# Score pairs on one PSUM tile and matmul bursts in a two-layer hybrid attention block

## The chip, the cores and the metric

The kernel runs on one core of a Trainium2 chip. The metric is the device time of one execution in microseconds. Three runs before the change took 1876.28, 1876.46 and 1880.62 us; their median is 1876.46 us.

## The reference

Two layers work on 512 latent tokens and 256 context tokens of width 1024. A layer normalises and modulates both streams, multiplies them by one input matrix, and sends the parts through four groups of heads; their outputs are joined, multiplied by an output matrix and added, and a SwiGLU network follows. The second layer needs no context output. What matters here is the attention of three groups:

```python
# A: windowed attention, 4 query heads on 2 key heads of width 64, a sink column
p = softmax(concat([where(|q-k| <= 128, qa @ ka.T, -1e30), qa @ ka_ctx.T, sink]))
# C: differential attention, 4 heads, each with two maps m of query/key width 32
p0, p1 = softmax(q[:, m] @ concat([k, k_ctx])[:, m].T)  for m in (0, 1)
y = rmsnorm((p0 - lam * p1) @ concat([v, v_ctx]))
# D: neighbourhood attention on an 8 x 64 grid, 4 heads of width 64, with a bias table
p = softmax(concat([qd @ kd_near.T + bias, qd @ kd_ctx.T]))
```

Context tokens of the first layer run the same groups against the 256 context keys alone. Group B is a convolution of 31 taps.

## The kernel before, in words

Large products are made of three matmuls in a short format (`mm3`, lines 162 to 164: high x high, high x low, low x high). The scores are split in the same way: a chain of three matmuls for each group of columns (`mm_rows`, line 613; written out in `d_attn`, lines 785 to 788).

The score work comes in pairs of chains on different rows of the array. In group C (`c_attn`, line 623) a pair is the two maps of one head for 128 queries, on 32 rows each: per map three matmuls over 512 latent keys and three over 256 context keys (only the latter for context queries). In A (`a_attn`, line 817) and D (`d_attn`, line 769) a pair is two heads on 64 rows each. Each chain of a pair writes a PSUM tile of its own: `self.ps("sc")` (768 columns, two buffers) or `self.ps("sd")` (512 columns, two buffers), line 639, 717, 778 and 830. VectorE then reads each tile with one instruction that copies the scores to SBUF and takes the row minimum (line 648, 796, 845; `ctx_attn` takes the minimum alone, line 726). ScalarE makes the exponentials (line 651, 734, 799, 848). The weights are scaled or combined, turned on TensorE by `tr_copy` (line 498, copied back in line 509 or 512), and multiplied with V in `pv` (line 599): two heads, their matmuls alternating over key tiles, one PSUM tile of which each head writes 64 partitions.

The attention steps are generators. `beside` (line 924) runs an attention generator and takes steps of side work, mostly projections of the next group (`proj_c`, `proj_d`, `proj_a`, through `unit`, lines 389 to 415), between its steps. In this manner the program's order is C of layer 0 with the projections of C and D beside it (about 136 to 306 us), D with the projections of A (to about 402), A with the loads of the output matrix (to about 470), and the same in layer 1 from about 1195 to 1452. The first three units of group B are made in `first_units` (line 427), two of them in `sc` tiles.

The order on each engine is not the program's order. The framework plans it before the kernel is compiled: it replays the instructions on a simulated timeline, and each engine takes the lowest number among those that are ready, where the number is the place in the program. A PSUM tile is taken by the first writer that is let go, and is given back after its last reader. The planned order is then fixed; on the chip an engine that has reached an instruction waits for it. `tc.high_priority(n)` lowers the numbers of what is written inside it by n.

Other tiles play a part in the argument: in lines 1027 to 1037, at the start of layer 0, transposes of two normalised token tiles write two tiles of 1024 columns, two token tiles taking turns (`for kk in range(4): for j in range(2)`).

Of the kernel before, what the change touches and what calls it, by code (L numbers as in the profile page):

```python
# [16 lines left out]
P = 128  # L17
D = 1024
NK = D // P
SEQ = 512  # L20
CTX = 256
NT = SEQ + CTX
# [28 lines left out]
class Hybrid:  # L51
# [19 lines left out]
    def tl(self, pool, shape, tag, bufs=1, dt=F32):  # L71
# [5 lines left out]
        "t": {"pt": (512, 2)},  # L77
        "x": {"ps": (1024, 3)},
        "u": {"pu": (512, 2)},
        "c": {"sc": (768, 2)},  # L80
        "e": {"sd": (512, 2), "ptd": (512, 2)},
    }

    def ps(self, tag="ps"):
# [11 lines left out]

    def dma(self, out, in_):
        self.nc.sync.dma_start(out, in_)  # L98

    def small(self, w, tag, bufs=8):  # L100
        return self.tl(self.smp, [P, w], tag, bufs)
# [325 lines left out]
    def first_units(self, l, H, c0s, nctx, by_k, between):  # L427
        w = self.t["w_in"][l]
        ws = [self.w_unit(w, c0) for c0 in c0s]
        outs = []  # L430
        for n in range(len(c0s)):
            if n < 2:
                a = self.ps("sc")
                outs.append((a[:, 0:512], a[:, 512:768] if nctx else None))
            else:
                outs.append((self.ps("pu"), self.ps("pu")[:, 0:256] if nctx else None))
        groups = [(0, 0, 256), (0, 256, 512)] if not by_k else [(0, 0, 512)]
        if nctx:
            groups.insert(0, (1, CTX0, CTX0 + 256))
        for g in [groups] if by_k else [[g] for g in groups]:  # L440
            self.abreast(ws, [[o[1] if x else o[0][:, a:b] for x, a, b in g] for o in outs], H, g, by_k)
            if between:
                between()
                between = None
        self.first = dict(zip(c0s, outs))
# [153 lines left out]
    def pv(self, parts, dest):  # L599

        nc = self.nc
        po = self.ps(self.pv_tag)
        n = len(parts[0])
        for i in range(n):
            for j in range(2):
                v, pt = parts[j][i]
                nc.tensor.matmul(po[64 * j:64 * j + 64, 0:P], v, pt, start=(i == 0), stop=(i == n - 1))  # L607
        src = po[:, 0:P]
        if len(dest.shape) == 3:
            src = src.rearrange("p (r c) -> p r c", r=dest.shape[1])  # L610
        nc.scalar.copy(dest, src)

    def mm_rows(self, outs, qs, ks, rows):

        for i, (a, b) in enumerate(((0, 0), (0, 1), (1, 0))):
            for o, q, k, r in zip(outs, qs, ks, rows):
                self.nc.tensor.matmul(o, q[a][r], k[b][r], start=(i == 0), stop=(i == 2))  # L617

    def blk(self, PT, i):
        return PT[:, i * P:(i + 1) * P]  # L620
# [2 lines left out]
    def c_attn(self, l, u):  # L623
        nc = self.nc
        q_ = self.lay[l]
        if u == 0:
            self.nblk = 0
            self.L0 = self.tl(self.cpool, [P, 6, 4], "L0", 1)
        L0 = self.L0
        Q, K = self.qkc["q", u], self.qkc["k", u]  # L630
        for n in range(6 if l == 0 else 4):
            lat = n < 4
            w = NT if lat else CTX
            nb = w // P
            PT = []
            for j in range(2):
                h = 2 * u + j
                rows = [slice(64 * j + 32 * m, 64 * j + 32 * m + 32) for m in range(2)]
                pss = [self.ps("sc") for _ in range(2)]
                qs = [[a[:, n * P:(n + 1) * P] for a in Q]] * 2  # L640
                for c0, c1, o in ((0, 512, 0), (512, NT, 512)) if lat else ((512, NT, 0),):
                    self.mm_rows([ps[:, o:o + c1 - c0] for ps in pss], qs, [[a[:, c0:c1] for a in K]] * 2, rows)
                Pm = []
                lm = self.small(1, "l1")
                for m in range(2):
                    nm = self.small(1, "nm")
                    Pm.append(self.a_s())
                    nc.vector.tensor_tensor_reduce(out=Pm[m][:, 0:w], in0=pss[m][:, 0:w],  # L648
                                                   in1=self.zcol.to_broadcast([P, w]),
                                                   scale=1.0, scalar=HUGE, op0=ALU.add, op1=ALU.min, accum_out=nm)  # L650
                    nc.scalar.activation(Pm[m][:, 0:w], Pm[m][:, 0:w], AF.Exp, scale=-1.0, bias=nm,
                                         accum_out=L0[:, n, h:h + 1] if m == 0 else lm)
                rl = self.small(1, "rl")
                nc.vector.reciprocal(rl, lm)
                cf = self.small(1, "cf")
                nc.vector.scalar_tensor_tensor(cf, L0[:, n, h:h + 1], q_["nlam"], rl, op0=ALU.mult, op1=ALU.mult)
                self.nblk += 1
                if l or self.nblk % 2 == 0:
                    nc.scalar.activation(Pm[1][:, 0:w], Pm[1][:, 0:w], AF.Copy, scale=cf)
                    nc.gpsimd.tensor_tensor(Pm[0][:, 0:w], Pm[0][:, 0:w], Pm[1][:, 0:w], op=ALU.add)  # L660
                else:
                    nc.vector.scalar_tensor_tensor(Pm[0][:, 0:w], Pm[1][:, 0:w], cf, Pm[0][:, 0:w],
                                                   op0=ALU.mult, op1=ALU.add)
                PT.append(self.a_pt())
                self.tr_copy([Pm[0][:, b * P:(b + 1) * P] for b in range(nb)], PT[j])
                yield
            self.pv([[(self.VC[:, kb, (2 * u + j) * 64:(2 * u + j) * 64 + 64], self.blk(PT[j], kb - 6 + nb))
                      for kb in range(6 - nb, 6)] for j in range(2)], self.yg["C"][:, u, n * P:(n + 1) * P])
# [45 lines left out]
    def ctx_attn(self, Q, K, vts, sinks, dest, tag):  # L714

        nc = self.nc
        pss = [self.ps(tag) for _ in range(2)]
        kc = [[a[:, SEQ:NT] for a in K]] * 2
        for e in range(2):
            qs = [[a[:, SEQ + e * P:SEQ + (e + 1) * P] for a in Q]] * 2  # L720
            self.mm_rows([ps[:, e * 256:(e + 1) * 256] for ps in pss], qs, kc, self.HALVES)
        PT = []
        for ps, sinkn in zip(pss, sinks):
            S = self.a_s()
# [44 lines left out]
    def d_attn(self, l, pool, u):  # L769
        nc = self.nc  # L770
        vh = lambda tb, j: self.VD[:, tb, (2 * u + j) * 64:(2 * u + j) * 64 + 64]
        Q, K = self.qkd["q", u], self.qkd["k", u]
# [2 lines left out]
        dest = yv[:, 0:SEQ].rearrange("p (r g c) -> p g r c", r=8, g=4)  # L775
        v2 = lambda a: a.rearrange("p (a k) -> p a k", a=2)
        for g in range(4):
            pss = [self.ps("sd") for _ in range(2)]
            qs = [[a[:, g * P:(g + 1) * P] for a in Q]] * 2

            def win(a):
                if g:
                    return a[:, (g - 1) * P:(g + 1) * P]
                return bass.AP(a.tensor, a[:, 3 * P:4 * P].offset, ap=[list(a.ap[0]), [-3 * P, 2], [1, P]])
            for o, f in ((0, win), (256, lambda a: a[:, SEQ:NT])):
                for i, (x, y) in enumerate(((0, 0), (0, 1), (1, 0))):
                    for j, r in enumerate(self.HALVES):
                        nc.tensor.matmul(pss[j][:, o:o + 256], qs[j][x][r], f(K[y][r]), start=(i == 0), stop=(i == 2))  # L788
            ty = (0, 1, 1, 2)[g]
            PT = []  # L790
            for j in range(2):
                n0 = nbs[j][:, ty].rearrange("p b k c -> p (b k c)")
                bias = bass.AP(n0.tensor, n0.offset, ap=[list(n0.ap[0]), [(3 - ty) * 256, 2], [1, 256]])
                S = self.a_s()
                nm = self.small(1, "dnm")
                nc.vector.tensor_tensor_reduce(out=v2(S[:, 0:512]), in0=v2(pss[j][:, 0:512]), in1=bias,
                                               scale=1.0, scalar=HUGE, op0=ALU.add, op1=ALU.min, accum_out=nm)
                ls = self.small(1, "dls")
                nc.scalar.activation(S[:, 0:512], S[:, 0:512], AF.Exp, scale=-1.0, bias=nm, accum_out=ls)
                PT.append(self.a_pt())  # L800
                self.soft_dst(S, 512, ls, PT[j], self.tr_tag)
                yield
            tbs = ((3, 0), (0, 1), (1, 2), (2, 3))[g] + (4, 5)
            self.pv([[(vh(tb, j), self.blk(PT[j], s)) for s, tb in enumerate(tbs)] for j in range(2)], dest[:, g])
# [12 lines left out]
    def a_attn(self, l, x):  # L817
        nc = self.nc
# [3 lines left out]
        Q, K = self.qka["q", x], self.qka["k"]  # L822
        sinks = [q_["sinkn"][:, 2 * g + x:2 * g + x + 1] for g in range(2)]
        yv = self.yg["A"][:, x]
        for n in range(4):
            lo, hi = max(0, n - 1), min(3, n + 1)
            wl = (hi - lo + 1) * P
            w = wl + CTX
            qs = [[a[:, n * P:(n + 1) * P] for a in Q]] * 2
            pss = [self.ps("sc") for _ in range(2)]  # L830
            self.mm_rows([ps[:, 512 - wl:512] for ps in pss], qs, [[a[:, lo * P:(hi + 1) * P] for a in K]] * 2, self.HALVES)
            self.mm_rows([ps[:, 512:768] for ps in pss], qs, [[a[:, SEQ:NT] for a in K]] * 2, self.HALVES)
            PT = []
            for g in range(2):
                S = self.a_s()
# [543 lines left out]
```

## Time and profile before

| what | us |
|---|---|
| median of three runs | 1876.46 |
| profiled execution | 1877.07 |
| its span, first to last instruction | 1875.3 |
| TensorE busy (matmuls) | 1785.0 |
| VectorE, ScalarE, GpSimd busy | 905.2, 679.4, 432.1 |

The mean granted TensorE clock of the execution is 0.968 of full speed. Matmuls are pipelined: the record of one lasts longer than the time until the next may start, so busy times of single groups of matmuls add up to more than the stretch; the distance from a run's first start to the start of the next instruction is what it costs TensorE.

### The profile page before, as it was taken

How to read it: one execution, taken by the hardware profiler on the slowest of the kernel's cores; microseconds unless marked ns; L12 is line 12 of the kernel's file. 1: busy time of each engine (PE TensorE's matmuls, PEld its weight loads, DVE VectorE, ACT ScalarE, POOL GpSimd, SP SyncE). 2: the span in 40 equal slices, each digit the busy share in tenths (PEclk: the TensorE clock that was granted, in tenths of full speed). 3: DMA queues.
4: the chain of work that ended last, by engine and by line, in shares of the span. 5: the costliest groups of instructions: out<-in, count | busy, mean ns of one | idle time of the engine just before them, and what ended most of it. 6: DMA issues, size and time to landing. Idle time of an engine off the chain costs nothing.

```text
span 1875.3 us, 28384 instructions
## 1 busy us (share of the span) xinstructions
PE 1785.0 (95%) x11812; PEld 1499.4 (80%) x11812; DVE 905.2 (48%) x1435; ACT 679.4 (36%) x1161; POOL 432.1 (23%) x324
## 2 busy tenths in 40 slices
PE   6897999988999999999999999899998999999997
PEld 5676888866788788888888888788986888888886
DVE  4668554475344334242434247754366444544443
ACT  4354555455233121112121225565455242222322
POOL 1587612352000000000100004883262000000002
PEclk8897999978999999999999999999998999999999
DMA  9341201213505353424141221121114353322421
GB/s 314 81 128 36 53 23 35 88 45 96 180 13 170 120 154 104 135 70 126 57 125 42 85 79 46 51 55 40 46 54 132 117 169 101 110 82 79 128 75 46
DMA packets 187983, 172.88 MB, mean 92 GB/s; under 512 B 17878, under 2 KB 150478, under 8 KB 187726
## 3 DMA queue, kind: packets, MB, share of 16 engines
q1 hardware_dynamic: 187854, 171.06, 29.9%
q8 instruction: 93, 1.52, 0.4%
q14 instruction: 36, 0.29, 0.1%
HBM read 166.76 MB, written 4.52 MB: 91 GB/s over the span
## 4 chain that ended last, share of the span: by engine, by line
PE 81%; POOL 5%; DVE 5%; DMA 3%; issue 2%; ACT 2%; SPq 1%; POOLq 0%; DVEq 0%; ACTq 0%
PE ps L162 18%; PE ps L163 18%; PE ps L164 18%; PE sc L617 4%; POOL accp L873 3%; PE pu L162 3%; PE pu L163 3%; PE pu L164 3%; PE pt L498 3%; PE pt L607 3%; PE ada L292 2%; DVE accd L881 1%; PE pu L607 1%; SPq L98 1%; PE sd L788 1%
## 5 line engine op out<-in xcount | busy, mean ns | idle before, releaser
L163 PE MATMUL ps<-h,whi 128*128 128x512 f32 (+1 forms) x1104 | 383.0, 348 | 1.6 <-DVE h L129 1.6
L162 PE MATMUL ps<-h,whi 128*128 128x512 f32 (+1 forms) x1104 | 382.4, 349 | 0.9 <-DVE gt L980 0.9
L164 PE MATMUL ps<-h,wlo 128*128 128x512 f32 (+1 forms) x1104 | 383.0, 348 | 0.0
L127 ACT CAST whi<-wraw 128x1024 fp32r<-128x1024 f32 (+1 forms) x132 | 134.5, 1023 | 409.5 <-PE ps L163 252.5
L129 DVE TENSOR_TENSOR wlo<-wraw,whi 128x1024 fp32r<-128x1024 f32 (+1 forms) x116 | 147.8, 1278 | 202.0 <-ACT whi L127 200.7
L163 PEld LDWEIGHTS ps<-h,whi 128*128 128x128 f32 x1104 | 208.9, 189 | 28.4 <-DVE h L129 2.0
L162 PEld LDWEIGHTS ps<-h,whi 128*128 128x128 f32 x1104 | 207.8, 189 | 29.7 <-issue 2.8
L164 PEld LDWEIGHTS ps<-h,wlo 128*128 128x128 f32 x1104 | 208.8, 189 | 27.8 <-issue 2.2
L162 PE MATMUL pu<-hT,whi 128*128 128x256 f32 (+1 forms) x648 | 199.8, 309 | 11.1 <-DVE hp L575 4.2
L983 POOL TENSOR_TENSOR x<-x,gt 128x1024 f32<-128x1024 f32 x12 | 29.7, 2476 | 728.5 <-DVE gt L980 728.5
L163 PE MATMUL pu<-hT,whi 128*128 128x256 f32 (+1 forms) x648 | 197.5, 305 | 0.0
L164 PE MATMUL pu<-hT,wlo 128*128 128x256 f32 (+1 forms) x648 | 196.5, 303 | 0.0
L162 PE MATMUL ps<-wdhi,zh 128*128 128x512 f32 x440 | 171.6, 392 | 0.4 <-ACT ntmp L367 0.4
L163 PE MATMUL ps<-wdlo,zh 128*128 128x512 f32 x440 | 171.0, 390 | 0.0
L164 PE MATMUL ps<-wdhi,zl 128*128 128x512 f32 x440 | 170.4, 391 | 0.0
L873 POOL TENSOR_TENSOR accp<-accp,cpr 128x783 f32<-128x783 f32 (+1 forms) x76 | 143.3, 1885 | 31.8 <-ACT cpr L872 26.0
L980 DVE TENSOR_TENSOR gt<-ps,g 128x1024 f32<-128x1024 f32 x66 | 80.6, 1223 | 134.9 <-PE ps L164 116.2
L127 ACT CAST wdhi<-wraw 128x1024 fp32r<-128x1024 f32 x44 | 46.2, 1055 | 270.2 <-PE ps L164 180.9
L162 PEld LDWEIGHTS pu<-hT,whi 128*128 128x128 f32 x648 | 125.9, 194 | 22.4 <-DVE hp L575 4.8
L163 PEld LDWEIGHTS pu<-hT,whi 128*128 128x128 f32 x648 | 126.2, 195 | 7.2 <-issue 2.4
L164 PEld LDWEIGHTS pu<-hT,wlo 128*128 128x128 f32 x648 | 126.1, 195 | 6.2 <-issue 1.9
L617 PE MATMUL sc<-qk,qk 32*128 32x256 f32 (+3 forms) x648 | 112.9, 343 | 8.9 <-DVE nm L648 5.9
(270 smaller groups left out, 2983.0 us busy)
## 6 DMA issues: line engine op xcount, KB each, us to landing
araw<-in_w_ada SPq DMA_DIRECT2D x60, 512.0 KB
wraw<-in_w_gate SPq DMA_DIRECT2D x44, 512.0 KB
wraw<-in_w_up SPq DMA_DIRECT2D x44, 512.0 KB
wraw<-in_w_down SPq DMA_DIRECT2D x44, 512.0 KB
wraw<-in_w_in SPq DMA_DIRECT2D x40, 512.0 KB
wraw<-in_w_ada SPq DMA_DIRECT2D x20, 512.0 KB
wraw<-in_w_out SPq DMA_DIRECT2D x12, 512.0 KB
whi<-in_w_ada SPq DMA_DIRECT2D x8, 512.0 KB
```

Source lines behind the costliest of these rows:

```text
L127: nc.scalar.copy(hi, src)
L129: eng.tensor_tensor(lo, src, f32(hi), op=ALU.subtract)
L162: mm(out, st[0], mv[0], start=first, stop=False)
L163: mm(out, st[0], mv[1], start=False, stop=False)
L164: mm(out, st[1], mv[0], start=False, stop=last)
L292: nc.tensor.matmul(ps[32 * j:32 * j + 32, 0:P], self.cstat[:, k, :], raw[:, a * 512 + j * P:a * 512 + (j + 1) * P], start=(k == 0), stop=( ...
L498: self.nc.tensor.transpose(pt[:, (i - a) * P:(i - a + 1) * P], blocks[i], self.ident)
L607: nc.tensor.matmul(po[64 * j:64 * j + 64, 0:P], v, pt, start=(i == 0), stop=(i == n - 1))
L617: self.nc.tensor.matmul(o, q[a][r], k[b][r], start=(i == 0), stop=(i == 2))
L873: nc.gpsimd.tensor_tensor(accp[:, 0:w], accp[:, 0:w], pr[:, 0:w], op=ALU.add)
L980: nc.vector.tensor_tensor(tmp, ps, g, op=ALU.mult)
L983: eng.tensor_tensor(x, x, tmp, op=ALU.add)
```

## The change

Tiles: `sc` becomes one buffer of 2048 columns and `sd` one buffer of 1024, and `ps2` hands out the two halves of such a tile, so that both chains of a pair (and two of the first units) share one tile. Bursts: the matmuls of a pair's scores, and those of a `pv`, are collected in a list; the first is issued with its ordinary number, all others under `high_priority(1 << 20)`. In `pv` the key tiles are taken from the last to the first.

```diff
-        "c": {"sc": (768, 2)},
-        "e": {"sd": (512, 2), "ptd": (512, 2)},
+        "c": {"sc": (2048, 1)},
+        "e": {"sd": (1024, 1), "ptd": (512, 2)},
+    def ps2(self, tag):
+        w = self.ptags[tag][0] // 2
+        a = self.ps(tag)
+        return [a[:, 0:w], a[:, w:2 * w]]
+    def burst_of(self, todo):
+        for n, f in enumerate(todo):
+            if n == 0:
+                f()
+            else:
+                with self.tc.high_priority(1 << 20):
+                    f()
...
# first_units
-        outs = []
+        outs, two = [], self.ps2("sc")
-                a = self.ps("sc")
+                a = two[n]
# pv
-        for i in range(n):
-            for j in range(2):
-                v, pt = parts[j][i]
-                nc.tensor.matmul(po[64 * j:64 * j + 64, 0:P], v, pt, start=(i == 0), stop=(i == n - 1))
+        self.burst_of([lambda i=i, j=j: nc.tensor.matmul(po[64 * j:64 * j + 64, 0:P], *parts[j][i], start=(i == n - 1),
+                                                         stop=(i == 0)) for i in reversed(range(n)) for j in range(2)])
# mm_rows hands back a list of the same matmuls in the same order
-        for i, (a, b) in enumerate(((0, 0), (0, 1), (1, 0))):
-            for o, q, k, r in zip(outs, qs, ks, rows):
-                self.nc.tensor.matmul(o, q[a][r], k[b][r], start=(i == 0), stop=(i == 2))
+        return [lambda o=o, q=q[a][r], k=k[b][r], i=i: self.nc.tensor.matmul(o, q, k, start=(i == 0), stop=(i == 2))
+                for i, (a, b) in enumerate(((0, 0), (0, 1), (1, 0))) for o, q, k, r in zip(outs, qs, ks, rows)]
# c_attn (ctx_attn, d_attn and a_attn alike)
-                pss = [self.ps("sc") for _ in range(2)]
+                pss = self.ps2("sc")
-                for c0, c1, o in ((0, 512, 0), (512, NT, 512)) if lat else ((512, NT, 0),):
-                    self.mm_rows([ps[:, o:o + c1 - c0] for ps in pss], qs, [[a[:, c0:c1] for a in K]] * 2, rows)
+                self.burst_of([f for c0, c1, o in (((0, 512, 0), (512, NT, 512)) if lat else ((512, NT, 0),)) for f in
+                               self.mm_rows([ps[:, o:o + c1 - c0] for ps in pss], qs, [[a[:, c0:c1] for a in K]] * 2, rows)])
```

## Rows read from the trace of the kernel before

**Rows 1.** The page, parts 1 and 4: busy time; the chain by engine.

```profile
PE 1785.0 (95%) x11812; PEld 1499.4 (80%) x11812; DVE 905.2 (48%) x1435; ACT 679.4 (36%) x1161; POOL 432.1 (23%) x324
...
PE 81%; POOL 5%; DVE 5%; DMA 3%; issue 2%; ACT 2%; SPq 1%; POOLq 0%; DVEq 0%; ACTq 0%
```

**Rows 2.** Busy time by stretch: stretch, length, PE, PEld, DVE, ACT, POOL, clock, DMA.

```profile
176.00:306.00 130.00, 130.00 (x992) 110.51 (x992) 69.23 (x163) 71.14 (x151) 52.63 (x39) 1.00 0.13 32
306.00:360.00 54.00, 54.00 (x458) 46.72 (x459) 22.44 (x59) 23.72 (x63) 16.70 (x23) 1.00 0.22 66
...
402.00:470.00 68.00, 59.25 (x569) 46.84 (x570) 43.85 (x134) 39.39 (x102) 23.40 (x23) 0.90 0.23 72
1216.00:1326.00 110.00, 108.78 (x863) 95.02 (x863) 52.46 (x112) 68.75 (x124) 63.76 (x47) 0.97 0.16 43
```

**Rows 3.** Chain by line: 176:306, 306:360, 402:470, 1216:1326, 1326:1380 (shares of the stretch).

```profile
by line: PE sc L617 27.8%; PE pu L162 17.3%; PE pu L163 16.5%; PE pu L164 15.8%; PE pt L607 11.5%; PE pt L498 10.7%; PE pt L457 0.7%
...
by line: PE pu L162 19.5%; PE pu L163 18.8%; PE pu L164 17.7%; PE pt L607 12.8%; PE sd L788 11.0%; PE ptd L498 9.2%; PE pt L498 4.9%; PE pt L457 3.2%; PE sd L617 2.2%; PE sc L617 0.8%
...
by line: PE pu L607 19.1%; PE sc L617 13.9%; PE pt L498 13.7%; PE pu L292 6.0%; DMA modg<-adab 4.5%; issue 4.4%; DMA adab<-in_b_ada 3.8%; DVE Pm L845 3.5%; DVE qk L906 2.9%; ACT Pm L734 2.8%; POOL Pm L813 2.8%; DVE nm L726 2.6%; POOL rs L10
...
by line: PE sc L617 19.0%; PE pu L163 13.6%; PE pu L162 13.6%; PE pu L164 12.8%; PE pt L498 8.8%; POOL accp L873 8.4%; PE pt L607 7.0%; issue 4.0%; POOL Pm L660 3.8%; POOL wlo L129 2.1%; ACT Pm L659 1.7%; ACT cpr L872 1.2%; ACT whi L127 0.9
...
by line: PE pu L162 18.6%; PE pu L164 18.2%; PE pu L163 17.7%; PE sd L788 14.7%; PE pt L498 13.0%; PE pt L607 12.3%; PE pt L457 5.1%; PE pu L681 0.8%
```

**Rows 4.** Timeline of TensorE: start, us, line, tiles, form of the first, count.

```profile
237.63 1.34 PE L617 MATMUL sc<-qk,qk 32*128 32x512 f32 x12
238.90 0.39 PE L162 MATMUL pu<-hT,whi 128*128 128x256 f32 x1
...
242.78 1.31 PE L617 MATMUL sc<-qk,qk 32*128 32x512 f32 x6
244.02 0.39 PE L164 MATMUL pu<-hT,wlo 128*128 128x256 f32 x1
...
291.64 0.63 PE L617 MATMUL sc<-qk,qk 32*128 32x256 f32 x6
292.21 0.39 PE L164 MATMUL pu<-hT,wlo 128*128 128x256 f32 x1
```

**Rows 5.** Groups by line and form: 176:306 (two), 1216:1326, 1326:1380.

```profile
L617 PE MATMUL sc<-qk,qk 32*128 32x512 f32 x75 | 22.2, 424 | 0.0
L617 PE MATMUL sc<-qk,qk 32*128 32x256 f32 x122 | 21.2, 294 | 0.0
...
L617 PE MATMUL sc<-qk,qk 32*128 32x512 f32 x81 | 20.1, 428 | 0.0
...
L788 PE MATMUL sd<-qk,qk 64*128 64x256 f32 x84 | 8.7, 299 | 0.0
```

**Rows 6.** Timeline of TensorE in group D.

```profile
367.00 0.98 PE L788 MATMUL sd<-qk,qk 64*128 64x256 f32 x12
367.91 1.12 PE L457 MATMUL pt<-rt,perm 128*128 128x512 f32 x2
```

**Rows 7.** VectorE's reads: timeline; groups of 176:306 and of 306:360.

```profile
238.97 0.96 DVE L648 CUSTOM_DVE_ANT_0 Pm<-sc,zcol 128x768 f32<-128x768 f32 x1 [1.61 <-PE sc L617]
...
L648 DVE CUSTOM_DVE_ANT_0 Pm<-sc,zcol 128x768 f32<-128x768 f32 (+1 forms) x41 | 30.7, 760 | 24.4 <-PE sc L617 15.6 <-POOL Pm L660 5.3 <-PE pt L498 3.0
...
L796 DVE CUSTOM_DVE_ANT_1 Pm<-sd,dnb 128x512 f32<-128x512 f32 x8 | 5.2, 689 | 9.8 <-PE sd L788 9.8
```

**Rows 8.** Timeline of TensorE at the start of layer 0.

```profile
18.86 0.69 PE L1034 MATMUL ps<-ident,xn 128*128 128x128 f32 x2 [0.98 <-DVE ss L338]
20.34 3.46 PE L1034 MATMUL ps<-ident,xn 128*128 128x128 f32 x15 [0.79 <-DVE ss L338]
```

**Rows 9.** Timeline of TensorE: PV runs.

```profile
203.59 1.53 PE L607 MATMUL pt<-PT,V 128*64 128x128 f32 x24
...
236.95 0.43 PE L607 MATMUL pt<-PT,V 128*64 128x128 f32 x2
```

More of the change, by code (lines that the diff above doesn't have):

```diff
@@ L716, in ctx_attn @@
         nc = self.nc
-        pss = [self.ps(tag) for _ in range(2)]
+        pss = self.ps2(tag)
         kc = [[a[:, SEQ:NT] for a in K]] * 2
-        for e in range(2):
-            qs = [[a[:, SEQ + e * P:SEQ + (e + 1) * P] for a in Q]] * 2
-            self.mm_rows([ps[:, e * 256:(e + 1) * 256] for ps in pss], qs, kc, self.HALVES)
+        qs = lambda e: [[a[:, SEQ + e * P:SEQ + (e + 1) * P] for a in Q]] * 2
+        self.burst_of([f for e in range(2) for f in
+                       self.mm_rows([ps[:, e * 256:(e + 1) * 256] for ps in pss], qs(e), kc, self.HALVES)])
         PT = []
@@ L777, in d_attn @@
         for g in range(4):
-            pss = [self.ps("sd") for _ in range(2)]
+            pss = self.ps2("sd")
             qs = [[a[:, g * P:(g + 1) * P] for a in Q]] * 2
@@ L784, in win @@
                 return bass.AP(a.tensor, a[:, 3 * P:4 * P].offset, ap=[list(a.ap[0]), [-3 * P, 2], [1, P]])
[L785 to L788, printed above, removed]
+            self.burst_of([lambda o=o, j=j, i=i, q=qs[j][x][r], k=f(K[y][r]): nc.tensor.matmul(
+                               pss[j][:, o:o + 256], q, k, start=(i == 0), stop=(i == 2))
+                           for o, f in ((0, win), (256, lambda a: a[:, SEQ:NT]))
+                           for i, (x, y) in enumerate(((0, 0), (0, 1), (1, 0))) for j, r in enumerate(self.HALVES)])
             ty = (0, 1, 1, 2)[g]
@@ L829, in a_attn @@
             qs = [[a[:, n * P:(n + 1) * P] for a in Q]] * 2
-            pss = [self.ps("sc") for _ in range(2)]
-            self.mm_rows([ps[:, 512 - wl:512] for ps in pss], qs, [[a[:, lo * P:(hi + 1) * P] for a in K]] * 2, self.HALVES)
-            self.mm_rows([ps[:, 512:768] for ps in pss], qs, [[a[:, SEQ:NT] for a in K]] * 2, self.HALVES)
+            pss = self.ps2("sc")
+            self.burst_of(
+                self.mm_rows([ps[:, 512 - wl:512] for ps in pss], qs, [[a[:, lo * P:(hi + 1) * P] for a in K]] * 2, self.HALVES)
+                + self.mm_rows([ps[:, 512:768] for ps in pss], qs, [[a[:, SEQ:NT] for a in K]] * 2, self.HALVES))
             PT = []
```

## The prediction

> **What bounds the kernel now.** I read the page's busy shares first, then the chain of waits, then both by stretch. TensorE is busy 95% of the span and carries 81% of the chain that ended last [rows 1]. That is a mean, so it says nothing about the attention code, which takes some 590 of the 1875 us: 136 to 470 in the first layer, 1195 to 1452 in the second. The table by stretch [rows 2] separates two kinds of attention time. In 176 to 306 and 1216 to 1326 (group C) and in 306 to 360 and 1326 to 1380 (group D) TensorE is busy throughout (130.00 of 130, 54.00 of 54, 108.78 of 110, and the fourth like the second) at a granted clock of 1.00 or 0.97, while VectorE is busy 69, 22 and 52 us. In 402 to 470 (group A) it is busy 59 of 68 us at 0.90: there waits count. The chains by line agree [rows 3]: in 176 to 306 every line named is TensorE, and the score matmuls of line 617 alone hold 27.8% of 130 us, 36.1 us.
>
> A score pair is two chains of matmuls on different rows of the array. The reader is to compare two runs of the timeline [rows 4]. At 237.63 both chains of a pair, 12 instructions, run side by side, and the next instruction starts 1.27 us later. At 242.78 one chain of 6 runs alone, and the next starts at 244.02: 1.24 us for half the work. One chain costs what two cost. So a pair whose chains come apart costs 2.48 us instead of 1.27, and TensorE has nothing to hide that under. They come apart because the two PSUM tiles come free one read apart: VectorE's read of one tile takes 0.96 us [rows 7], and the planner puts the first chain into the first freed tile and other work (line 162 to 164) between it and the second.
>
> **The change, part by part.** *One tile for a pair, issued as a burst.* It adds no instruction and removes none; both chains now wait for one release, and eleven of twelve matmuls have a number that puts them ahead of all else that is ready. I take every pair as a run like that at 237.63.
>
> 176 to 306: 75 matmuls of 512 columns and 122 of 256 [rows 5]. A latent pair has six of each, so there are 75/6 = 12.5 latent pairs, and (122 - 75)/6 = 7.8 context pairs. Side by side they cost 12.5 x 1.27 + 7.8 x 0.57 (291.64 to 292.21 [rows 4]) = 20.4 us. Now they hold 36.1. Saved: 15.7.
>
> 1216 to 1326: 81/6 = 13.5 latent pairs [rows 5], 17.1 us side by side. Now: at least the 20.9 us that line 617 holds on the chain (19.0% of 110 [rows 3]), at most 13.5 x 2 x 1.24 = 33.5 if no pair ran together. I take 24, nearer the chain's row, because what lies off the chain need not pay. Saved: 6.9, between 3.8 and 16.4.
>
> Group D: a pair is 12 matmuls of 256 columns and costs 0.91 together (367.00 to 367.91 [rows 6]). In 306 to 360 the score lines hold 11.0 + 2.2 + 0.8 = 14.0% of 54 us, 7.6; 74 instructions (60 of line 788 and 14 of line 617) are 6.2 pairs, 5.6 us. In 1326 to 1380 they hold 14.7%, 7.9; 84 instructions [rows 5] are 7 pairs, 6.4 us. Saved: 2.0 + 1.5 = 3.5.
>
> Group A and the ends of D: not saturated. Line 617 holds 13.9% of 68 us, 9.5, in 402 to 470 [rows 3]; halved, 4.7, and as much again in the second layer, so at most +10. Against it stands what the shared tile takes away: today the next pair's first chain may start after one read, then only after both. That is one read per pair, 0.69 to 0.96 us [rows 7], for 18 pairs: at worst -17. I take +3, near nothing, because there the row that ends last is as often a transpose, a PV run or a DMA as a score.
>
> *Does the burst keep its order?* The first matmul of a burst keeps its ordinary number; only the other eleven jump. If those of the second chain could go without the first, the pair would come apart again. That hangs on whether the planner keeps the writes to one tile in the program's order. For another tile it does [rows 8]: lines 1030 to 1034 write two tiles of 1024 columns (two PSUM banks each), taking turns between two inputs, and while only the first input was there, two transposes ran, one per tile, and then TensorE sat idle 0.79 us for the second input. Transposes of the first input into other columns and the other bank of the same tiles were ready and did not go. So writes to one tile keep their order, and the chains of a shared tile will follow the first matmul one by one. Before, the chains had separate tiles and no such order.
>
> *PV in reverse, as a burst.* The two heads' PV matmuls alternate on one tile. Some runs start with two instructions alone and the rest follows later: at 236.95 two take 0.43 us, where 24 in one run take 1.53, 0.06 each [rows 9]. Such a split costs 0.43 - 0.13 = 0.3 us. Starting from the last key tile makes the first two wait for the later copy of the transposed weights, after which all are ready; it does not stop the first instruction from going alone, as it hangs on the first head. I take +1 us, from 0 (nothing changes) to 3 (all splits go, some ten).
>
> *first_units* now draws its two units from one tile; in both layers they are written in the program's order already and read after it. Nothing, and no cover is needed: the tile is next used some 50 us later.
>
> Sum: 15.7 + 6.9 + 3.5 + 3 + 1 = 30 us. The profiled execution took 1877.07 us (span 1875.3 and 1.8 around it); the median of the runs shown is 1876.46. 1877 - 30 = 1847, and by the median 1846. What is late next in the C stretches is still TensorE: 130 - 16 = 114 us against VectorE's 69.
>
> One rule of the Trainium skill speaks against this. The page TensorEngine Tiling (Performance Considerations, PSUM Bottleneck) says that tiling speeds up TensorE but not the emptying of PSUM, which may then bind. No number of the sum needs it; the rows put the reads at 30.7 us of VectorE in 176 to 306 (41 reads of 0.76 [rows 7]), far below 114, so as throughput it does not bind. As latency it is the last rival below.
>
> **Rivals.**
> *Half is given back.* With TensorE quicker, VectorE and ScalarE come later in the pair's own chain: 1.3 us of scores, two reads of 0.96 and then exp, transposes and PV, and the tile is free only after both reads. For: 1216 to 1326 already has POOL accp 8.4%, issue 4.0% and POOL Pm 3.8% on its chain. Against: a cycle of scores and reads is 1.3 + 1.9 = 3.2 us and a pair has 130/20.3 = 6.4 us now, 5.6 afterwards. Half of 30: 1862.
> *Nothing changes,* since the planner's timeline is not the chip's, and bursts end up where runs of 6 were: 1876. Against: pairs whose tiles are both free run together today (237.63).
> *The second chain goes ahead of the first.* If writes to separate banks of the shared tile are not ordered, the eleven go at once, less the first chain's three wide ones. A latent pair then costs 1.24 + two thirds of 1.24 = 2.07, a D pair 2 x 0.91 = 1.82. 12.5 x 2.07 + 7.8 x 2 x 0.57 = 34.8 against 36.1; 13.5 x 2.07 = 27.9 against 24; 13.2 x 1.82 = 24.0 against 15.5. Together 11 us slower: 1888. Against: the idle time of [rows 8].
> *TensorE stands still for the second read.* The tile is given back one read later, and a burst ahead of everything in TensorE's queue makes all behind it wait: the next projection matmuls, and the transposes that VectorE and ScalarE wait for. Price if it happens at every pair of the four saturated stretches: 33.8 pairs x 1.0 us (the read and its semaphore) + 13.2 x 0.69 = 43 us, less the 26 saved: 17 slower, 1894. It decides from 26/47 = 0.55 us of standstill per pair. Against: in 176 to 306 scores are 36 of TensorE's 130 busy us, so there is other work to put between. For: the planner's order is fixed before the chip's times are known. This is the rule of the Trainium skill above, as a wait.
>
> **How the numbers follow.** Forecast 0.62 (own range 1834 to 1858: the savings' ends 3.8 and 16.4, and group A's); half given back 0.16; nothing 0.08; second chain ahead 0.08; standstill 0.06. Range 1832 to 1878: the low end takes every upper bound in part, the high end takes in half and nothing; outside lie the two slower rivals, 0.14, and some 0.05 below. The measurement can tell 0.3%, 5.6 us, from no change. Faster: 0.62 + 0.16, less 0.01 for a half that shrinks, 0.77. Same: 0.09. Slower: 0.14.
>
> **What would show it.** Right: nearly all score runs of the C stretches are of 12 (or 6 of 256 columns, at 0.57 us), next instruction 1.27 us on; line 617's share of those chains near 20 of 114 and 17 of 103 us; the C stretch of the first layer shorter by some 14 us. Wrong: runs of 9 and of 3; TensorE idle before line 617 until VectorE's reads; stretches as long as before though the runs are of 12. The forecast fails if the A stretches grow by over 15 us.

## The result and the profile after

The changed kernel takes 1833.65 us (median of four runs, 1833.23 to 1834.63) against 1878.29 us before, run beside it: 0.9763 of the time, 95% interval 0.9746 to 0.978. That is 44.6 us faster; 30 were forecast. 1833.65 lies near the low end of the range, and just below the 1834 to 1858 that the prediction gave its own forecast.

Two lines of the page, to set against [rows 1]: TensorE is busy 62 us less and carries a smaller part of the chain.

```profile
PE 1722.9 (94%) x11812; PEld 1456.6 (80%) x11812; DVE 904.9 (49%) x1435; ACT 673.9 (37%) x1161; POOL 435.0 (24%) x324
...
PE 75%; DVE 7%; POOL 6%; issue 3%; DMA 3%; ACT 3%; SPq 2%; POOLq 0%; ACTq 0%; DVEq 0%
```

Busy time by stretch (columns as in [rows 2]). The stretches are chosen so that they hold about as many matmuls (the x behind PE) as those of before (in D and A some 4 and 5% fewer): group C, layer 0; D; A; C, layer 1.

```profile
169.50:284.00 114.50, 111.28 (x993) 98.67 (x993) 73.70 (x163) 73.09 (x156) 59.54 (x42) 1.00 0.14 37
284.00:332.00 48.00, 48.00 (x441) 42.06 (x441) 21.83 (x61) 23.45 (x63) 16.79 (x24) 1.00 0.24 74
370.00:435.00 65.00, 50.40 (x539) 38.65 (x540) 41.85 (x130) 37.90 (x100) 21.17 (x22) 0.87 0.25 77
1182.00:1282.00 100.00, 95.58 (x857) 85.64 (x858) 52.92 (x116) 68.06 (x124) 64.07 (x47) 1.00 0.18 47
```

993 matmuls now take 114.5 us where 992 took 130; 857 take 100 where 863 took 110. TensorE is no longer busy without a gap in the C stretches: 3.2 and 4.4 us are idle, where 0 and 1.2 were. The chain by line of the first stretch names what is late next:

```profile
by line: POOL accp L886 13.5%; PE pu L177 12.1%; PE pu L178 11.8%; PE pu L179 11.5%; PE sc L628 11.0%; issue 7.6%; PE pt L513 7.3%; PE pt L619 7.0%; DVE Pm L660 2.8%; ACT Pm L663 2.7%; POOL wlo L144 2.5%; DVE cf L668 2.1%; POOL rt L476 2.0%
```

The scores (line 628, formerly 617) fell from 27.8% of 130 us [rows 3] to 11.0% of 114.5. The largest single line is now the taps of the convolution on GpSimd (accp). TensorE's lines together still hold most of the chain, as the prediction said, and VectorE, at 73.7 of 114.5 us, holds little.

Timeline of TensorE (start, us, line, tiles, first form, count), to set against [rows 4, 6]: a latent pair, a context pair and a D pair, each with the instruction behind it.

```profile
235.25 1.31 PE L628 MATMUL sc<-qk,qk 32*128 32x512 f32 x12
236.49 0.44 PE L513 MATMUL pt<-ident,Pm 128*128 128x128 f32 x2
...
270.64 0.62 PE L628 MATMUL sc<-qk,qk 32*128 32x256 f32 x6
271.19 0.39 PE L179 MATMUL pu<-hT,wlo 128*128 128x256 f32 x1
...
288.68 0.98 PE L797 MATMUL sd<-qk,qk 64*128 64x256 f32 x12
289.59 0.39 PE L177 MATMUL pu<-hT,whi 128*128 128x256 f32 x1
```

They cost 1.24, 0.55 and 0.91 us, close to the prices used in the prediction (1.27, 0.57, 0.91). Of 130 score runs before, 25 had 12 matmuls; of 79 now, 66 do. The groups of line 628 by form in 169.5 to 284 (busy us, mean ns, then idle before it and its releaser) answer to [rows 5]:

```profile
L628 PE MATMUL sc<-qk,qk 32*128 32x512 f32 x78 | 12.6, 425 | 1.0 <-DVE nm L660 1.0
L628 PE MATMUL sc<-qk,qk 32*128 32x256 f32 x120 | 11.5, 290 | 1.3 <-DVE nm L660 1.3
```

About as many matmuls (78 for 75, 120 for 122), each as long as before (425 against 424 ns), keep TensorE busy for 12.6 instead of 22.2 us (512 columns) and 11.5 instead of 21.2 (256), because two are in the array at once. Their wait for VectorE's reads is 2.3 us in this stretch. Over the whole execution the idle time before the scores of `sc` (behind the second bar) did not grow; the first line is of the kernel before:

```profile
L617 PE MATMUL sc<-qk,qk 32*128 32x256 f32 (+3 forms) x648 | 112.9, 343 | 8.9 <-DVE nm L648 5.9
L628 PE MATMUL sc<-qk,qk 32*128 32x256 f32 (+3 forms) x648 | 68.1, 337 | 8.3 <-DVE nm L660 6.7 <-DVE nm L858 1.5
```

**Where TensorE's time went.** For every run below, each matmul is given the time from its start to the next one's start, or to its own end if that is earlier; the rest, from the first matmul to the last, is idle. Of what falls into stretches at the lower clock, half is counted as work and half as loss to the clock. "Scores" is the part of the work in score matmuls.

| kernel | ratio to before (95%) | scores | all work | lost to half clock | idle |
|---|---|---|---|---|---|
| before, two profiles | 1 | 125.9, 125.3 | 1738.7, 1738.3 | 45.9, 50.6 | 74.9, 74.9 |
| changed, two profiles | 0.9763 (0.9746 to 0.978) | 79.6, 79.3 | 1688.3, 1686.7 | 34.1, 34.7 | 92.2, 92.8 |
| e1 scores only | 0.974 (0.9712 to 0.9768) | 78.7 | 1686.0 | 39.5 | 89.7 |
| e2 PV only | 0.9987 (0.9967 to 1.0006) | 129.1 | 1741.8 | 43.6 | 74.7 |
| e3 tile only | 0.9814 (0.9789 to 0.9839) | 86.4 | 1695.0 | 37.6 | 94.9 |
| e4 burst only | 0.9961 (0.9945 to 0.9977) | 126.7 | 1736.6 | 44.2 | 74.5 |
| e5 C only | 0.978 (0.9765 to 0.9795) | 97.1 | 1704.2 | 41.3 | 77.3 |
| e6 C and D | 0.9759 (0.9744 to 0.9774) | 89.8 | 1696.0 | 39.7 | 82.3 |
| e7 chain after chain | 0.985 (0.9835 to 0.9865) | 109.6 | 1715.9 | 40.9 | 78.2 |
| e8 PV second head first | 0.9714 (0.9698 to 0.973) | 78.7 | 1669.2 | 41.5 | 99.4 |
| e9 and projection bursts of 24 | 0.9717 (0.9699 to 0.9736) | 78.4 | 1671.0 | 43.3 | 96.9 |
| e10 the same, of 12 | 0.9711 (0.9688 to 0.9734) | 78.3 | 1670.7 | 42.5 | 98.3 |

The changed kernel has 51 us less work (46 of it scores) and loses 14 us less to the clock; 18 us come back as idle time. That makes 47, and the profiled spans differ by 46.

### The profile page after: what moved, and what is told of

It is laid out like the page before. It is cut to its first block, busy times and chain, and to the rows that moved or that the text cites. A ratio compares the mean times of both kernels' runs of the same rounds, so it can differ in the third digit from the quotient of the medians.

```text
span 1831.8 us, 28387 instructions
## 1 busy us (share of the span) xinstructions
PE 1722.9 (94%) x11812; PEld 1456.6 (80%) x11812; DVE 904.9 (49%) x1435; ACT 673.9 (37%) x1161; POOL 435.0 (24%) x324
## 4 chain that ended last, share of the span: by engine, by line
PE 75%; DVE 7%; POOL 6%; issue 3%; DMA 3%; ACT 3%; SPq 2%; POOLq 0%; ACTq 0%; DVEq 0%
PE ps L177 18%; PE ps L178 18%; PE ps L179 18%; POOL accp L886 4%; PE pu L178 3%; PE pu L177 3%; PE pu L179 3%; PE pt L513 2%; PE pt L619 2%; SPq L98 2%; PE sc L628 2%; PE ada L307 2%; DVE accd L894 1%; PE pu L619 1%; DVE wlo L144 1%
## 5 line engine op out<-in xcount | busy, mean ns | idle before, releaser
L177 PEld LDWEIGHTS ps<-h,whi 128*128 128x128 f32 x1104 | 208.4, 190 | 29.8 <-issue 2.6
L177 PE MATMUL pu<-hT,whi 128*128 128x256 f32 (+1 forms) x648 | 197.0, 304 | 8.2 <-DVE qk L147 3.3
L178 PE MATMUL pu<-hT,whi 128*128 128x256 f32 (+1 forms) x648 | 193.7, 299 | 0.0
L886 POOL TENSOR_TENSOR accp<-accp,cpr 128x783 f32<-128x783 f32 (+1 forms) x76 | 145.6, 1915 | 19.8 <-ACT cpr L885 13.9
L177 PEld LDWEIGHTS pu<-hT,whi 128*128 128x128 f32 x648 | 123.9, 191 | 17.0 <-DVE qk L147 3.8
L178 PEld LDWEIGHTS pu<-hT,whi 128*128 128x128 f32 x648 | 124.1, 191 | 5.7 <-issue 2.4
L1259 DVE TENSOR_TENSOR sg<-sg,ps 128x768 f32<-128x768 f32 (+1 forms) x44 | 36.1, 820 | 143.8 <-PE ps L179 123.0
```

Source lines behind the costliest of these rows:

```text
L177: mm(out, st[0], mv[0], start=first, stop=False)
L178: mm(out, st[0], mv[1], start=False, stop=False)
L886: nc.gpsimd.tensor_tensor(accp[:, 0:w], accp[:, 0:w], pr[:, 0:w], op=ALU.add)
```

## The experiments

**Which part does it.** Four kernels take the change apart. PV keeps its old form in e1, e3 and e4.

e1, the new scores with the old PV:

```diff
-        self.burst_of([lambda i=i, j=j: nc.tensor.matmul(po[...], *parts[j][i], ...) for i in reversed(range(n)) for j in range(2)])
+        for i in range(n):
+            for j in range(2):
+                nc.tensor.matmul(po[64 * j:64 * j + 64, 0:P], *parts[j][i], start=(i == 0), stop=(i == n - 1))
```

> Only the score half of the change: shared tile and burst for the score pairs, PV matmuls as before. Theory (the gain comes from the two chains of a pair running side by side): 1834 us, within 4 us of the changed kernel, and nearly all score runs have 12 matmuls that cost 1.25 us. Rival (a good part comes from the PV order): 1850 us or more.

Measured: 1831.82 us, 0.974. The scores carry the whole gain. The runs are 68 of 12 and 8 of 6 matmuls, one for each pair of the program.

e2, the new PV with the old scores: of the change, this hunk alone.

```diff
-        for i in range(n):
-            for j in range(2):
...
+        self.burst_of([lambda i=i, j=j: nc.tensor.matmul(...) for i in reversed(range(n)) for j in range(2)])
```

> Only the PV half of the change: reverse key tiles and burst; scores on separate tiles as before. Theory (PV gives nothing, because the first matmul of a PV still goes ahead alone with the first head): within 4 us of the kernel before, 1874 to 1880 us. Rival (PV order carries the 15 us by which the forecast was short): 1860 us.

Measured: 1878.76 us, 0.9987, and the interval reaches from 0.9967 to 1.0006: no gain that can be told from none.

e3, the tile without the burst:

```diff
     def burst_of(self, todo):
-        for n, f in enumerate(todo):
-            ... (all but the first under high_priority)
+        for f in todo:
+            f()
```

> Shared tile for the score pairs, but no burst: all matmuls keep their ordinary numbers; PV as before. Theory (one tile keeps the two chains in the order of the program, so they stay interleaved; other work may still cut a pair in two, at some 0.1 to 0.2 us a cut): 1840 us, between 1834 and 1850. Rival (the burst does it, the tile alone nothing): 1870 us or more.

Measured: 1845.5 us, 0.9814. The tile alone gives some 35 of the 49 us of e1. The timeline of TensorE in this kernel shows a cut pair:

```profile
231.17 1.31 PE L626 MATMUL sc<-qk,qk 32*128 32x512 f32 x11
232.41 0.44 PE L509 MATMUL pt<-ident,Pm 128*128 128x128 f32 x2
232.78 0.43 PE L618 MATMUL pt<-PT,V 128*64 128x128 f32 x2
233.15 0.38 PE L626 MATMUL sc<-qk,qk 32*128 32x256 f32 x1
233.46 0.39 PE L173 MATMUL pu<-hT,whi 128*128 128x256 f32 x1
```

Eleven matmuls run side by side and the twelfth comes 0.74 us later, for 0.31 us more. A cut pair stays in order and loses a little; only 43 of the 103 score runs have all 12 matmuls.

e4, the burst without the tile:

```diff
-        "c": {"sc": (2048, 1)},
-        "e": {"sd": (1024, 1), "ptd": (512, 2)},
+        "c": {"sc": (768, 2)},
+        "e": {"sd": (512, 2), "ptd": (512, 2)},
     def ps2(self, tag):
-        w = self.ptags[tag][0] // 2
-        a = self.ps(tag)
-        return [a[:, 0:w], a[:, w:2 * w]]
+        return [self.ps(tag) for _ in range(2)]
```

> Burst for the score pairs, but every chain on a tile of its own as before, two buffers; PV as before. Theory (tiles come free one read apart, so the first chain still runs alone and the second later, 2.48 us a pair): 1870 us, between 1860 and 1880, with most score runs of 6 matmuls. Rival (the burst does it): 1834 to 1845 us.

Measured: 1872.61 us, 0.9961. 67 of 115 score runs have 6 matmuls, 32 have 12. The timeline of TensorE shows a pair of it come apart:

```profile
241.78 1.32 PE L628 MATMUL sc<-qk,qk 32*128 32x512 f32 x6
243.03 0.43 PE L620 MATMUL pt<-PT,V 128*64 128x128 f32 x2
...
244.54 1.31 PE L628 MATMUL sc<-qk,qk 32*128 32x512 f32 x6
245.78 0.39 PE L176 MATMUL pu<-hT,whi 128*128 128x256 f32 x1
```

The second chain starts 2.76 us after the first, and they cost 1.25 and 1.24 us. A high place in the order does not bring the chains together while each has a tile of its own.

What parts them is the planned order, and not a wait on the chip. In the kernel before, VectorE's two reads ahead of the pair at 242.78 [rows 4, 7] end at 239.93 and 240.80, so both tiles are free 2 us before the first chain starts; the second starts at 244.46 all the same:

```profile
239.85 0.95 DVE L648 CUSTOM_DVE_ANT_0 Pm<-sc,zcol 128x768 f32<-128x768 f32 x1
...
244.46 1.31 PE L617 MATMUL sc<-qk,qk 32*128 32x512 f32 x6
```

That the planner's replay saw the two tiles come free one read apart is the likely reason for this order; its simulated times are not on record.

**Which stage.** In e5 and e6 the other groups keep two tiles and their ordinary order:

```diff
+        "a": {"sc": (768, 2)},                 # group A's own tiles, in e5 and e6
+        "e": {"sd": (512, 2), "ptd": (512, 2)},  # e5 alone
     def ps2(self, tag):
+        w, n, _ = self.ptags[tag]
+        self.shared = n == 1
+        if n == 2:
+            return [self.ps(tag) for _ in range(2)]
...
     def burst_of(self, todo):
-            if n == 0:
+            if n == 0 or not self.shared:
...
-        self.psum_push("c")
+        self.psum_push("a")                    # ahead of group A
```

> Shared tile and burst in group C alone (and the shared tile in the first units); groups D and A with two tiles and ordinary order as before; PV as before. By the prediction's terms for C (15.7 + 6.9): 22.6 us faster than before. Rival (the terms were too small, because pairs outside 176 to 306 and 1216 to 1326 and the half clock were counted at nothing): 30 us or more faster than before.

Measured: 1839.36 us against 1881.33, 0.978: group C alone gives 41 us (39 to 44), nearly twice its term. The rival is right.

> Shared tile and burst in groups C and D, group A (its context part too) with two tiles and ordinary order as before; PV as before. By the prediction's terms 26 us faster than before, and within 3 us of the kernel with all score pairs shared. Rival (group A's shared tile costs idle time that two tiles would not): faster than the kernel with all score pairs shared. Second rival (group A's pairs carry part of the surplus): 8 us or more slower than that kernel.

Measured: 1835.51 us, 0.9759: D adds 4 us (forecast 3.5); the intervals of the ratios overlap, but all four runs of e6 are below all four of e5, which ran beside it. To e1, which has A's pairs too, another 3.6 us are missing by the ratios, again with intervals that overlap. The rivals expected A to cost time or to give 8 us or more, and neither shows. The stretch from the last read of D's latent scores to the last PV of the first layer, in e6 and then in e1 (columns as before), tells why A gives so little:

```profile
358.00:436.60 78.60, 68.77 (x637) 54.24 (x636) 50.17 (x154) 45.95 (x120) 27.46 (x26) 0.88 0.19 55
```

```profile
355.20:433.80 78.60, 61.80 (x641) 47.17 (x644) 50.08 (x156) 45.80 (x121) 26.56 (x26) 0.89 0.22 69
```

Sharing takes 7.0 us of TensorE's busy time out of this stage, and the stage is as long as before, 78.6 us: TensorE isn't what it waits for.

**Does the alternation matter, or only that the chains are neighbours?** e7 queues one chain behind the other:

```diff
-    for i, (a, b) in enumerate(((0, 0), (0, 1), (1, 0))) for o, q, k, r in zip(outs, qs, ks, rows)
+    for o, q, k, r in zip(outs, qs, ks, rows) for i, (a, b) in enumerate(((0, 0), (0, 1), (1, 0)))
```

and in the same way all of the first chain's column groups before the second's.

> Shared tile and burst for all score pairs, but within a burst the six matmuls of the first chain come before the six of the second; PV as before. Theory (only matmuls that alternate between the two row groups run side by side): 2 x 1.24 us a latent pair, some 1870 us. Rival (one release and one burst are enough, and TensorE runs neighbouring chains on different rows beside each other by itself): 1832 to 1845 us, pairs at 1.3 to 1.7 us.

Measured: 1852.9 us, 0.985, between the two. The theory is refuted: neighbours overlap without alternating, though less. The timeline shows 1.81 us a pair (234.28 to 236.09), between 1.24 and 2.48:

```profile
234.28 1.88 PE L630 MATMUL sc<-qk,qk 32*128 32x512 f32 x12
236.09 0.38 PE L179 MATMUL pu<-hT,wlo 128*128 128x256 f32 x1
```

The groups of the first 0.8 us of that run, 234.27 to 235.10, by form:

```profile
L630 PE MATMUL sc<-qk,qk 32*128 32x512 f32 x4 | 1.1, 441 | 0.0
...
L630 PE MATMUL sc<-qk,qk 32*128 32x256 f32 x1 | 0.3, 273 | 0.0
```

A chain has three matmuls of 512 columns and then three of 256. Four of 512 have started when there is one of 256: the second chain's first matmul has started ahead of at least two matmuls of the first chain that stand before it in the queue. In the program built from this kernel all six of one chain stand ahead of all six of the other in every pair, so the planner did not mix them; in the trace, in all 32 latent pairs, four matmuls of 512 columns start before the first of 256.

**A better PV.** In e8 each PV begins with the second head:

```diff
-    for i in reversed(range(n)) for j in range(2)])
+    for i in reversed(range(n)) for j in (1, 0)])
```

> The changed kernel, except that each PV begins with the second of its two heads, whose weights come last, so that no matmul can go ahead alone. Theory (every split PV costs 0.3 us of TensorE, some 25 of them): 5 to 8 us faster than the changed kernel. Rival (a split costs nothing, because the next matmul would have waited or the split only moves idle time): within 2 us of the changed kernel.

Measured: 1828.73 us, 0.9714 (0.9698 to 0.973), 4.9 us below the changed kernel by the medians and 9 by the ratio, whose intervals just part; in time, the theory's 5 to 8 is met. The PV groups of line 619 in 134 to 433, first in the changed kernel, then in e8:

```profile
L619 PE MATMUL pt<-PT,V 128*64 128x128 f32 x224 | 17.4, 279 | 0.2 <-DVE PT L527 0.2
```

```profile
L619 PE MATMUL pt<-PT,V 128*64 128x128 f32 x224 | 14.9, 278 | 0.0
```

In the changed kernel 22 PV runs are two instructions alone (27 before); in e8 none is. The theory's sum does not hold, though. Over the whole execution the PV matmuls of all groups take 64.4 us of work instead of 79.3, and their runs fall from 81 to 56: 0.6 us a run, twice the price in the theory. All work falls by 18 us, of which 7 come back as idle and 7 as half clock, and what is left happens to be near the forecast.

e9 and e10 add bursts to e8: the 24 matmuls of a projection of one group of columns as one burst, or (e10, `k % 4 == 3`) as two of 12.

```diff
     def unit(...):
-                self.mm3(o, st, mv, k == 0, k == NK - 1)
+                todo += [...]            # the three matmuls of mm3, as functions
+                if k % 8 == 7:
+                    self.burst_of(todo)
+                    todo = []
```

> The changed kernel with the second head of each PV first, and in addition the 24 matmuls of a projection of one group of columns (line 177 to 179, called from unit) as one burst. Theory (each change from one kind of matmul to another costs some 0.1 us at both sides, and this takes some 45 of the cuts out of the projections): 5 to 9 us faster than the same kernel without projection bursts, about 1821 us. Rival (a burst of 24 lasts 2.7 us, and the transposes and scores behind it come later, so that TensorE is idle afterwards): as fast or slower than without.

> As the kernel with projection bursts, but in bursts of 12 (1.4 us). Theory (cuts cost 0.2 us each; some 20 fewer): 2 to 4 us faster than without projection bursts. Rival (bursts delay what waits behind them): as fast or slower, but less so than with bursts of 24.

Measured: 1827.66 and 1827.02 us, 0.9717 (0.9699 to 0.9736) and 0.9711 (0.9688 to 0.9734): the same as e8. The theory fails for both in time. Its price is right, but not what follows: against e8, the projections' matmuls in e9 take 8.9 us less, while the transposes and the permutations (`perm`, line 457 before) take 9.9 us more. Why these cost more behind a burst is open. e10 is the lowest median here, but not clear of e8, so e8 is the version to keep.

**Is the clock's part chance?** Second profiles of the kernel before and of the changed one:

> The kernel before once more, for a second profile. If the half-clock time of TensorE belongs to the kernel, the matmuls again lose about 46 us to it over the whole span, 32 of them in the attention. If it is a matter of the single execution, the figure differs by 10 us or more.

> The changed kernel once more, beside the two kernels with projection bursts, and for a second profile. About 1834 us. If the smaller half-clock loss belongs to the change, the matmuls again lose about 34 us to it, 17 of them in the attention; if it is a matter of the single execution, the figure comes nearer to that of the kernel before.

Measured: 50.6 us lost before (45.9 in the first profile) and 34.7 after (34.1). The second profile of before took 1881.29 us, and the changed kernel 1833.61 (0.9751, interval 0.9733 to 0.9769). So the smaller loss belongs to the change, though single profiles of one kernel differ by up to 5 us. The granted clock of all executions says the same: 0.961 to 0.970, mean 0.965, in 37 executions of the kernel before that ran beside the experiments, and 0.972 to 0.975, mean 0.973, in eight of the changed kernel. It is not the shared tile alone: e2 and e4, whose pairs still come apart, have a mean of 0.969 in ten executions each.

The start of group C in the first layer shows the difference best. The stretch 136 to 180 of e11, e4, e12 and e1 (the number behind POOL's count is the granted clock):

```profile
136.00:180.00 44.00, 31.28 (x165) 26.84 (x166) 39.39 (x38) 20.21 (x31) 34.78 (x16) 0.69 0.13 38
```

```profile
136.00:180.00 44.00, 31.26 (x186) 27.15 (x185) 39.55 (x43) 22.14 (x36) 34.60 (x15) 0.77 0.12 36
```

```profile
136.00:180.00 44.00, 32.17 (x251) 29.14 (x250) 41.48 (x45) 23.46 (x39) 35.41 (x16) 0.84 0.13 37
```

```profile
136.00:180.00 44.00, 32.99 (x270) 30.38 (x269) 39.77 (x47) 25.63 (x41) 37.16 (x16) 0.88 0.13 37
```

With pairs apart (the first two) the mean clock is 0.69 and 0.77, with pairs together 0.84 and 0.88. All profiles part in this way: 0.69 to 0.77 in the four profiles of kernels without the shared tile (before twice, e2, e4), where TensorE starts 162 to 191 matmuls in these 44 us, and 0.84 to 0.88 in the ten with it, with 233 to 270 matmuls.

## Why the prediction was right, and where it was 15 us short

*The mechanism* held for the score pairs. A pair on one tile costs what the one run at 237.63 cost [rows 4]; writes to one tile keep the program's order, as read from [rows 8] (e1's runs are the program's pairs, one for one, and even without the burst e3 keeps the order); it is the tile, more than the burst, that brings the chains together (e3 gives 35 us, e4 some 7, both together 49). One reading needs a limit: the two tiles coming free one read apart is not what parts a pair on the chip, where both were free at 240.80; it can only have acted in the planner's replay.

*"Saved: 15.7"* for 176 to 306: the work in score matmuls, counted as in the table, fell from 36.1 to 20.7 us, by 15.4. Right.

*"Saved: 6.9, between 3.8 and 16.4"* for 1216 to 1326: 8.4, from 26.1 to 17.7 us. A little too small: the 24 us were taken near the chain's row, yet scores off the chain saved time too. The stretch is 10 us shorter because 3.4 us of loss to the half clock and 1.4 us of other work went as well, while idle time grew by 3.2.

*Group D, 3.5:* 4 (e6 against e5), but by luck. D's score work fell by 7.3 us, twice the term, because pairs outside 306 to 360 and 1326 to 1380 gained too, and 5.0 us came back as idle time, for which the term had nothing. *Group A, +3 from -17 and +10:* 3.6 (e1 against e6), which is not clear of noise; the two prices behind it are there, 11.1 us less score work and 7.4 more idle.

*PV, +1:* nothing shown (e2: 0.9987; the changed kernel against e1: 0.9763 against 0.974, with intervals that overlap). The reason given in the prediction is right: the first matmul hangs on the first head. That starting with the other head would remove the split was within reach of that sentence; e8 shows it.

*The step that failed is the sum for C:* 22.6 forecast, 41 measured (e5). It counted only scores, and only inside the two saturated stretches. Against the mean of the two profiles of before, e5 has 28.5 us less score work, 5.8 less other work, 7.0 less loss to the clock and 2.4 more idle: 38.9, which is the difference of the profiled spans. Beyond the 22.6, and with the 2 us of idle time taken off:
- 6 us are scores: some 5 are pairs outside the two stretches, the rest is the 6.9 that should have been 8.4. In all, C's scores fell from 43.3 to 24.5 us in the first layer and from 29.8 to 19.8 in the second.
- 6 us are projections and transposes that did not change. The likely reason, not tested by itself, is that fewer score runs (96 for 130) mean fewer changes of kind. In the first profile of before, at full clock, the matmul behind a projection matmul starts 0.12 us after it (median) in a run of projections, 0.22 if a score run stands ahead of the two, and 0.20 if a transpose does; a score run starts 0.21 after the projection matmul ahead of it, a transpose 0.12. In e5, 33 fewer projections follow on a score run, 19 fewer score runs follow on a projection, and 10 more projections follow on a transpose: at these prices some 4 of the 6 us, an estimate. The Trainium skill says on the page TensorEngine Tiling (Tiling Modes, Key Properties) that changing the tiling mode drains TensorE. The trace agrees ahead of a score run (0.21 against 0.12 ahead of a transpose, which like a projection has the form 128*128); behind one, 0.22 is hardly more than the 0.20 behind a transpose, so that this delay is not shown to come from the mode.
- 7 us are the clock, for which the sum had no term. The figure is rough, since two profiles of the same kernel differ by 5; but all four executions of e5 have a granted clock of 0.970 to 0.973, against a mean of 0.965 before. In the whole change it is 14 us. What keeps the clock up was not isolated, and e2 and e4 show that a part of it comes without pairs on one tile.

*The rivals.* Half given back: of 65 us less work and clock loss, 18 came back as idle, some 28%, not half. Nothing changes: refuted. The second chain ahead of the first: does not happen on a shared tile with the changed kernel's order. TensorE stands still for the second read: 2.3 us in the first C stretch (line 628's idle before it), 0.11 for each of some 20 pairs, where 0.55 would have decided; over the whole execution this idle time did not grow (8.9 before, 8.3 after).

## What to carry to other kernels

Where two matmul chains are to share the array, give them one release: one PSUM tile, and then one place in the order. Size such a change by all the time that the doubled work holds, not by its share of one chain in one stretch; expect some of it back as idle time where TensorE is not the limit; and give the clock a term of its own, since the granted clock moved with the change here (0.965 to 0.973). If a burst's first member hangs on an early input, start it with the member whose input comes last.

## What was not expected of the hardware

Two chains on different rows overlap even when queued one behind the other: 1.81 us for a pair in e7 (1.79 to 1.84 for all whole latent pairs at full clock), where alternating takes 1.24 (1.24 to 1.26 in the changed kernel) and two chains apart 2.48. The second chain's first matmul starts ahead of matmuls that were queued before it. The page TensorE: Matmul & The Clock Gate of the Trainium skill (Part 3, The mechanism) says that only weight loads are pulled ahead and that matmuls start strictly in queue order; e7 differs, and the measurement decides here.
